# Seven-product FFN up stage in a written-out order, with the split of f moved to the down stage and eight PSUM banks for the two plain pairs

## Chip, core and metric

The kernel runs on one core of one Trainium2 chip. The metric is the device time of one execution in microseconds (us). Engines are named as in the profile: PE (TensorE matmul), PEld (its weight loads), DVE (VectorE), ACT (ScalarE), POOL (GpSimd), SP (SyncE, which here only issues loads). A name with a "q" behind it (SPq, POOLq) is that engine's queue issuing a DMA.

## What is computed

One layer of a decoder trunk on x of 1024 x 1024, float32: token mixing (dilated attention in three groups, a gated convolution branch, a gated merge, an output projection, RMSNorm), and then the channel-mixing part, which is all that the change touches:

```python
h = rms_norm(x, norm_ffn_pre[layer])
u = h @ w_up[layer].astype(h.dtype)                         # 1024 x 1024 by 1024 x 5632
u = causal_depthwise_conv(u, ffn_conv_w[layer], ffn_conv_b[layer])   # 3 taps along the sequence
u_gate, u_val = jnp.split(u, 2, axis=-1)                    # 2816 each
f = jax.nn.gelu(u_gate, approximate=True) * u_val
y = f @ w_down[layer].astype(f.dtype)                       # 1024 x 2816 by 2816 x 1024
x = x + rms_norm(y, norm_ffn_post[layer])
```

## The kernel before, in words

**Products.** Every float32 operand is split into a high part (fp32r) and a low part (the rest), and a product is the sum of three matmuls: high by high, high by low, low by high. `split` (L188 to L194) makes the parts of a weight tile: an ACT copy writes `wh` (L192), a DVE subtraction writes `wl` (L193). `wh` and `wl` have 7 buffers each.

**Up stage.** The 2816 gate and 2816 value channels are taken in 22 blocks j of 128. For one j the transposed output (256 channels by 1024 positions) is a 2 x 2 arrangement of 128 x 512 quarters, and so are its weights (`quadrant`, L714, 256 KB each, loaded by SP) and its input (the quarters B11, B21, B12, B22 of the normed and transposed h, in four chunks k). Two blocks, j = 0 and 1, are made plainly (`up_plain`, L732): eight products of 512 rows each for a block, each 12 matmuls of 128 x 512 (`product`, L723). The other 20 use seven products instead of eight (`class Seven`, L747), on sums of the quarters: T1 to T4 of the input (made once, `strassen_rows`, L150) and s1 to s4 of the weights (made by POOL for each block, L757 to L760, in `ws` tiles). I call the products of a block P1 (weights a11, L764), P5 (s1, L767), P2 (a12, L772), P6 (s2, L774), P7 (s3, L778), P3 (s4, L782) and P4 (a22, L784).

**The accumulators.** A block has one PSUM tile `pp` of 128 x 1024, with two buffers in turn. Its halves are `b1` (P1, P2, P3) and `b2` (P5, P6, P7, P4). Between the products partial results are copied out or from one half to the other: after P5 `gate` high half <- b2 (L768) and b2 <- b1 (L769); after P2 `gate` low half <- b1 (L773); after P6 b1 <- b2 (L775), all on ACT; after P7 `val` high half = b2 + gate (L779, DVE); after P3 `gate` high half += b1 (L783, DVE); after P4 `val` low half <- b2 (L785, ACT).

**Behind the products** (`gated`, L698): for the gate and the value tile an ACT scale and bias (L691) and two DVE taps (L694), then gelu on ACT (L701), a DVE product (L702), the split of f on ACT and DVE (L703, L704), and two stores of both parts into a scratch in DRAM (L706).

**Plain pairs.** Outputs of j = 0 take both halves of two `pp` tiles, those of j = 1 the two `ps` banks; a weight is loaded and split again for each half h of the positions. The results are copied into `u` tiles (L743), which live in the pool `ffn`; that pool takes the memory of the pool `res`, in which the input sums T1 to T4 are formed.

**Down stage** (`down`, L822): for each half of the positions, 22 steps k; SP loads both parts of f (512 KB, L829) and two weight quarters (L833), and 24 matmuls (L212 to L214) accumulate into all eight banks.

**What sets the order.** Before the change a scheduler puts the instructions of each engine in an order of its own by a timeline that it estimates. On the chip each engine's queue then runs in that order, and waits on semaphores for what comes from other engines.

Of the kernel before, what the change touches and what calls it, by code (L numbers as in the profile page):

```python
# [11 lines left out]
F32 = mybir.dt.float32  # L12
F32R = mybir.dt.float32r
# [65 lines left out]
def trunk_kernel(ctx: ExitStack, tc: tile.TileContext, a, out):  # L79
# [14 lines left out]
    def ps_tile(shape=(P, 512), tag=None):  # L94

        if tag is None:
            tag = ("ps", "pt", "ps", "po")[banks[0] % 4]
            banks[0] += 1
        return psum.tile(list(shape), F32, tag=tag, name=tag, bufs=2 if tag == "ps" else 1)
# [7 lines left out]
    def f(ap):  # L107
        return ap.bitcast(F32)
# [21 lines left out]
    def rsqrt_of(ss, scale, eps, pool, tag, n=1):  # L130
# [15 lines left out]
                nc.vector.tensor_mul(t, t, h)  # L146
            nc.vector.scalar_tensor_tensor(y, t, 1.5, y, op0=ALU.subtract, op1=ALU.mult)
        return y

    def strassen_rows(b11, b21, pt12, pt22, gain12, gain22, temp, make):  # L150

        def parts(x):
            t = make()
            nc.scalar.copy(t[:, 0], x)
            nc.vector.tensor_sub(t[:, 1], x, f(t[:, 0]))
            return t

        b12, b22 = temp("x12"), temp("x22")  # L160
        nc.scalar.activation(b12, pt12, AF.Copy, scale=gain12)
        nc.scalar.activation(b22, pt22, AF.Copy, scale=gain22)
        out = {"B22": parts(b22), "B12": parts(b12)}
        t1, t3, t2 = temp("x1"), temp("x3"), temp("x2")
        nc.gpsimd.tensor_sub(t3, b22, b12)
        nc.vector.tensor_sub(t1, b12, f(b11[:, 0]))
        nc.vector.tensor_sub(t1, t1, f(b11[:, 1]))
        out["T1"] = parts(t1)
        out["T3"] = parts(t3)
        nc.vector.tensor_sub(t2, b22, t1)  # L170
        out["T2"] = parts(t2)
        nc.vector.tensor_sub(t2, f(b21[:, 0]), t2)
        nc.vector.tensor_add(t2, t2, f(b21[:, 1]))
        return out, lambda: parts(t2)

    def transposed(rows, parts, gain, tag=None):

# [49 lines left out]
    with ExitStack() as mix:  # L227
# [372 lines left out]
        with tc.tile_pool(name="res", bufs=1) as res:  # L600
# [18 lines left out]
            for h in range(2):  # L619
# [32 lines left out]
                if h == 0:  # L652
# [1 line left out]
                        h2T[k] = dt(F32R, (P, 2, 512))  # L654
                    transposed(h2, lambda k: (h2T[k][:, 0], h2T[k][:, 1]), ffn_g)
                    continue
                temps = {"x12": ("xr", 0), "x22": ("xr", 1), "x1": ("oc", 0), "x2": ("oc", 1)}
                last = []
                for k in range(4):
                    pair = [ps_tile((P, 4, P), tag) for tag in ("pt", "po")]  # L660
                    for n, pt in enumerate(pair):
                        for t in range(4):
                            c = (k + 4 * n) * P
                            nc.tensor.transpose(pt[:, t, :], h2[t][:, c:c + P], ident)
                    wide = {"xr": nat2("xr", 2), "oc": nat2("oc", 1)}
                    third = res.tile([P, 512], F32, tag="x3", name="x3", bufs=2)

                    def temp(name):
                        if name == "x3":
                            return third  # L670
                        tag, n = temps[name]
                        return wide[tag][:, n * 512:(n + 1) * 512]

                    p12, p22 = (pt.rearrange("p a b -> p (a b)") for pt in pair)
                    more, t4 = strassen_rows(h2T[k], h2T[k + 4], p12, p22, ffn_g[:, k:k + 1],
                                             ffn_g[:, k + 4:k + 5], temp, lambda: dt(F32R, (P, 2, 512)))
                    for name, tile_ in more.items():
                        X[name, k] = tile_
                    X["B11", k], X["B21", k] = h2T[k], h2T[k + 4]
                    X["T4", k] = t4()  # L680


    with tc.tile_pool(name="ffn", bufs=1) as ffn:
        fscr = dram.tile([NF, 2, P, 2, 512], F32, name="fscr")

        def u_tile():
            return ffn.tile([P, S], F32, tag="u", name="u", bufs=6)

        def conv3(src, c):
            o = u_tile()  # L690
            nc.scalar.activation(o, src, AF.Identity, scale=ffn_w[:, c, 2:3], bias=ffn_b[:, c:c + 1])  # L691
            for k in (1, 0):
                d = 2 - k
                nc.vector.scalar_tensor_tensor(o[:, d:], src[:, :S - d], ffn_w[:, c, k:k + 1], o[:, d:],  # L694
                                               op0=ALU.mult, op1=ALU.add)
            return o

        def gated(j, gate, val):  # L698

            og, ov = conv3(gate, j), conv3(val, NF + j)  # L700
            nc.scalar.activation(og, og, AF.Gelu_apprx_tanh)  # L701
            nc.vector.tensor_mul(og, og, ov)  # L702
            nc.scalar.copy(ov.bitcast(F32R), og)  # L703
            nc.vector.tensor_sub(og.bitcast(F32R), og, ov)  # L704
            for n, src in enumerate((ov, og)):
                nc.gpsimd.dma_start(fscr[j, :, :, n, :].rearrange("h p c -> p h c"),  # L706
                                    src.rearrange("p (h c) -> p h c", h=2))

        def raw_tile(early=False):
            if early:  # L710
# [21 lines left out]
        def up_plain(js):  # L732

            us = {(j, c): u_tile() for j in js for c in range(2)}
            pps = {c: pp_tile() for c in range(2)}
            for h in range(2):
                for n, j in enumerate(js):
                    for c in range(2):
                        ps = pps[c][:, h * 512:(h + 1) * 512] if n == 0 else ps_tile(tag="ps")
                        for kh in range(2):  # L740
                            product(ps, wsplit(quadrant(j, 2 * c + kh)), ("B11", "B21", "B12", "B22")[2 * h + kh], kh == 0, kh == 1)
                        dst = us[j, c][:, h * 512:(h + 1) * 512]
                        (nc.vector.tensor_copy if c else nc.scalar.copy)(dst, ps)  # L743
            for j in js:
                gated(j, us[j, 0], us[j, 1])

        class Seven:  # L747

            def __init__(self, j):
                self.j = j
                self.a11, self.a21, self.a22, self.a12 = (quadrant(j, q) for q in (0, 2, 3, 1))
                self.s = [ffn.tile([P, 512], F32, tag="ws", name="ws", bufs=4) for _ in range(4)]
                s1, s2, s3, s4 = self.s
                nc.gpsimd.tensor_add(s1, self.a21, self.a22)  # L757
                nc.gpsimd.tensor_sub(s2, s1, self.a11)
                nc.gpsimd.tensor_sub(s3, self.a11, self.a21)
                nc.gpsimd.tensor_sub(s4, self.a12, s2)  # L760
                both = pp_tile()
                self.b1, self.b2 = both[:, 0:512], both[:, 512:1024]
                self.gate, self.val = u_tile(), u_tile()
                product(self.b1, wsplit(self.a11), "B11", True, False, True)  # L764

            def fifth(self):
                product(self.b2, wsplit(self.s[0]), "T1", True, False, True)  # L767
                nc.scalar.copy(self.gate[:, 512:1024], self.b2)  # L768
                nc.scalar.copy(self.b2, self.b1)  # L769

            def second(self):
                product(self.b1, wsplit(self.a12), "B21", False, False, True)  # L772
                nc.scalar.copy(self.gate[:, 0:512], self.b1)  # L773
                product(self.b2, wsplit(self.s[1]), "T2", False, False, True)  # L774
                nc.scalar.copy(self.b1, self.b2)  # L775

            def seventh(self):
                product(self.b2, wsplit(self.s[2]), "T3", False, False, True)  # L778
                nc.vector.tensor_add(self.val[:, 512:1024], self.b2, self.gate[:, 512:1024])  # L779

            def last(self):
                product(self.b1, wsplit(self.s[3]), "B22", False, False, True)  # L782
                nc.vector.tensor_add(self.gate[:, 512:1024], self.b1, self.gate[:, 512:1024])  # L783
                product(self.b2, wsplit(self.a22), "T4", False, False, True)  # L784
                nc.scalar.copy(self.val[:, 0:512], self.b2)  # L785
                gated(self.j, self.gate, self.val)

        up_plain((0, 1))
        now = Seven(2)
        now.fifth()  # L790
        for j in range(2, NF):
            now.second()
            then = Seven(j + 1) if j + 1 < NF else None
            now.seventh()
            if then:
                then.fifth()
            now.last()
            now = then


        post = dt()
# [20 lines left out]
        def down(h, late=3):  # L822
# [2 lines left out]
            banks += [[ps_tile(tag="ps") for _ in range(2)], [ps_tile(tag=tag) for tag in ("pt", "po")]]  # L825

            def load(k):
                ft = dt(F32R, (P, 2, 512))
                nc.sync.dma_start(f(ft), fscr[k, h])  # L829
                w = []  # L830
                for cs in cols:
                    raw = raw_tile()
                    nc.sync.dma_start(raw, a["w_down"][k * P:(k + 1) * P, cs])  # L833
                    w.append(wsplit(raw))
                return ft, w
# [87 lines left out]
```

## Time and profile before

| what | us |
|---|---|
| median of 3 runs (1889.32 to 1891.16) | 1889.87 |
| the profiled execution | 1892.74 |
| its span, first to last instruction | 1891.0 |
| PE busy in the span | 1782.0 |
| DVE busy | 1187.2 |
| ACT busy | 720.7 |
| POOL busy | 217.7 |

A row of the timeline has the start, the duration, the engine, the line, the operation, what it writes <- reads and a count of merged instructions; in brackets stands how long the engine was idle before and which instruction released it. Matmuls overlap, so one of 390 ns starts every 227 ns when PE is fed. PEclk is the granted clock of TensorE: 1.00 is 2.4 GHz, 0.50 is 1.2 GHz.

### The profile page before, as it was taken

What the parts mean: (1) busy time and instruction counts of PE and PEld (TensorE: products, weight loads), DVE (VectorE), ACT (ScalarE), POOL (GpSimd) and SP (SyncE); (2) the same over time, 40 slices, a digit from 0 to 9 for tenths busy, and PEclk for the clock granted to TensorE, in tenths of its full rate; (3) what the DMA queues carried; (4) which work ended last, traced back from release to release, by engine and by line L of the source; (5) the groups of instructions that cost most, each with busy time, mean ns of one, the idle gap of its engine ahead of it and who ended that gap; (6) DMA issues with size and microseconds to landing.
All of it is one profiled execution on the core that took longest, in us unless ns stands there. A gap on an engine that the chain in (4) does not pass through costs nothing. (4 is left out here: it accounts for less than half of the span.)

```text
span 1891.0 us, 22339 instructions
## 1 busy us (share of the span) xinstructions
PE 1782.0 (94%) x8152; PEld 1488.4 (79%) x8152; DVE 1187.2 (63%) x1956; ACT 720.7 (38%) x1312; POOL 217.7 (12%) x211
## 2 busy tenths in 40 slices
PE   7799998999999999999999994899999999999997
PEld 5688898888888888888888883777777777888886
DVE  6249978367752969657644578766666666532624
ACT  6132343333323342223432444455454545422322
POOL 0000000111100000000000001433333333000000
PEclk9899999999999999999999997999999999999999
DMA  5312132112321222354331431432222232885522
GB/s 188 105 48 59 48 93 79 52 53 61 90 61 54 57 68 89 101 175 131 98 112 59 148 125 48 135 102 109 90 100 89 90 122 89 309 325 172 181 92 101
DMA packets 87246, 203.68 MB, mean 108 GB/s; under 512 B 11347, under 2 KB 13283, under 8 KB 87136
## 3 DMA queue, kind: packets, MB, share of 16 engines
q1 hardware_dynamic: 72000, 159.42, 26.4%
q0 software_dynamic: 11888, 39.26, 6.2%
q10 hardware_dynamic: 3248, 3.58, 0.6%
q8 instruction: 64, 1.05, 0.2%
q14 instruction: 46, 0.38, 0.1%
HBM read 155.93 MB, written 48.38 MB: 108 GB/s over the span
## 5 line engine op out<-in xcount | busy, mean ns | idle before, releaser
L212 PE MATMUL pp<-d,wh 128*128 128x512 f32 x1088 | 429.8, 395 | 15.9 <-DVE d L358 15.6
L729 PE MATMUL pp<-d,wh 128*128 128x512 f32 x1184 | 377.2, 400 | 61.7 <-DVE u L779 31.9
L214 PE MATMUL pp<-d,wl 128*128 128x512 f32 x1088 | 428.8, 394 | 0.0
L213 PE MATMUL pp<-d,wh 128*128 128x512 f32 x1088 | 428.7, 394 | 0.0
L729 PEld LDWEIGHTS pp<-d,wh 128*128 128x128 f32 x1184 | 226.5, 193 | 118.1 <-DVE u L779 40.0
L297 DVE SCALAR_TENSOR_TENSOR acc<-cin,conv_w,acc 128x1024 f32<-128x1024 f32 x240 | 304.9, 1279 | 4.5 <-issue 1.4
L212 PEld LDWEIGHTS pp<-d,wh 128*128 128x128 f32 x1088 | 206.0, 189 | 58.7 <-issue 16.6
L193 DVE TENSOR_TENSOR wl<-wr,wh 128x512 fp32r<-128x512 f32 x207 | 142.2, 691 | 162.5 <-ACT wh L192 162.1
L214 PEld LDWEIGHTS pp<-d,wl 128*128 128x128 f32 x1088 | 206.1, 189 | 41.7
L213 PEld LDWEIGHTS pp<-d,wh 128*128 128x128 f32 x1088 | 206.1, 189 | 41.2
L729 PE MATMUL pp<-d,wl 128*128 128x512 f32 x592 | 235.4, 398 | 0.0
L192 ACT CAST wh<-wr 128x512 fp32r<-128x512 f32 x207 | 127.7, 621 | 279.4 <-PE pp L213 164.3
L193 DVE TENSOR_TENSOR wl<-wq,wh 128x512 fp32r<-128x512 f32 x148 | 122.2, 832 | 148.0 <-ACT wh L192 146.6
L192 ACT CAST wh<-wq 128x512 fp32r<-128x512 f32 x148 | 91.8, 623 | 221.3 <-PE pp L214 119.3
L694 DVE SCALAR_TENSOR_TENSOR u<-u,ffn_w 128x1023 f32<-128x1023 f32 x88 | 113.7, 1292 | 53.0 <-ACT u L691 53.0
L729 PEld LDWEIGHTS pp<-d,wl 128*128 128x128 f32 x592 | 114.3, 193 | 24.6
L192 ACT CAST wh<-ws 128x512 fp32r<-128x512 f32 x80 | 49.3, 618 | 119.8 <-PE pp L729 119.8
L212 PE MATMUL pp<-wh,d 128*128 128x512 f32 x232 | 90.2, 391 | 0.7 <-ACT oc L637 0.7
L213 PE MATMUL pp<-wl,d 128*128 128x512 f32 x232 | 90.4, 390 | 0.0
L214 PE MATMUL pp<-wh,d 128*128 128x512 f32 x232 | 90.4, 390 | 0.0
L351 PE MATMUL pp<-wh,d 128*128 128x512 f32 x192 | 79.5, 415 | 3.0 <-DVE d L358 3.0
L352 PE MATMUL pp<-wl,d 128*128 128x512 f32 x192 | 78.3, 408 | 0.0
(282 smaller groups left out, 2549.9 us busy)
## 6 DMA issues: line engine op xcount, KB each, us to landing
fscr<-u POOLq DMA_DIRECT2D x44, 512.0 KB, 4.9
d<-fscr SPq DMA_DIRECT2D x44, 512.0 KB, 7.2
wq<-in_w_down_dram SPq DMA_DIRECT2D x88, 256.0 KB, 3.1
wq<-in_w_up_dram SPq DMA_DIRECT2D x80, 256.0 KB, 3.2
wr<-in_w_v_dram SPq DMA_DIRECT2D x48, 256.0 KB, 2.8
wr<-in_w_qk_dram SPq DMA_DIRECT2D x48, 256.0 KB, 2.7
wr<-in_w_glu_dram SPq DMA_DIRECT2D x32, 256.0 KB, 2.7
wr<-in_w_gate_dram SPq DMA_DIRECT2D x32, 256.0 KB, 2.8
```

The lines of the kernel that those rows point to most:

```text
L192: nc.scalar.copy(hi, raw)
L193: nc.vector.tensor_sub(lo, raw, f(hi))
L212: nc.tensor.matmul(ps, lh, rh, start=first, stop=False)
L213: nc.tensor.matmul(ps, lh, rl, start=False, stop=False)
L214: nc.tensor.matmul(ps, ll, rh, start=False, stop=last)
L297: nc.vector.scalar_tensor_tensor(acc, cin[:, k:k + S], conv_w[:, m, k:k + 1], acc, op0=ALU.mult, op1=ALU.add)
L351: nc.tensor.matmul(ps, hTh[k][:, sl], wh, start=k == 0, stop=False)
L352: nc.tensor.matmul(ps, hTh[k][:, sl], wl, start=False, stop=False)
L694: nc.vector.scalar_tensor_tensor(o[:, d:], src[:, :S - d], ffn_w[:, c, k:k + 1], o[:, d:], op0=ALU.mult, op1=ALU.add)
L729: nc.tensor.matmul(ps, wp[:, cs], xp, start=first and k == 0 and n == 0, stop=last and k == 3 and n == 2, skip_group_check=open_)
```

## The change

- **Order.** The up stage of the 20 blocks is no longer left to the scheduler. `Seven.steps` gives each action a slot (`AT` for the products, one product a slot, seven slots a block) and a rank in it (product and the copies behind it 0, loads 1, weight split 2, POOL sums 3, what follows the products 4). All actions are sorted by slot, rank and block, and issued under `tc.manual_schedule()`, which keeps each engine's queue in the issued order. A weight is split five slots ahead of its product; a22 is loaded a second time. The order of products stays P2, P6 of a block, P1 of the next, P7, P5 of the next, P3, P4.
- **f.** L703 and L704 are gone from the up stage; f goes to the scratch once, as float32 (512 KB for each block in place of 1 MB), and the down stage loads 256 KB for a step and splits it there, on ACT and DVE, out of a `ws` tile.
- **Plain pairs.** j = 1 uses `ps`, `ps` in the first half of positions and `pt`, `po` in the second. Seven of the eight split weights are kept for the second half.
- **Input sums.** B12 and B22 of all four chunks are made first, in `d` tiles, and T1 to T4 after them, with two `xr` buffers in place of one `oc`.

```diff
-                temps = {"x12": ("xr", 0), "x22": ("xr", 1), "x1": ("oc", 0), "x2": ("oc", 1)}
...
+                        x = wide[k][:, n * 512:(n + 1) * 512]
+                        nc.scalar.activation(x, pt.rearrange("p a b -> p (a b)"), AF.Copy, scale=ffn_g[:, c:c + 1])
+                        X[("B12", "B22")[n], k] = parts(x)
...
+                for k in range(4):
+                    b12, b22 = wide[k][:, 0:512], wide[k][:, 512:1024]
+                    both = nat2("xr", 2)
+                    t1, t3 = both[:, 0:512], both[:, 512:1024]
+                    nc.vector.tensor_sub(t1, b12, f(h2T[k][:, 0]))
+                    nc.vector.tensor_sub(t1, t1, f(h2T[k][:, 1]))
+                    X["T1", k] = parts(t1)
+                    nc.gpsimd.tensor_sub(t3, b22, b12)
+                    X["T3", k] = parts(t3)
+                    nc.vector.tensor_sub(t1, b22, t1)
+                    X["T2", k] = parts(t1)
+                    nc.vector.tensor_sub(t1, f(h2T[k + 4][:, 0]), t1)
+                    nc.vector.tensor_add(t1, t1, f(h2T[k + 4][:, 1]))
+                    X["T4", k] = parts(t1)
...
-            nc.scalar.copy(ov.bitcast(F32R), og)
-            nc.vector.tensor_sub(og.bitcast(F32R), og, ov)
...
-                        ps = pps[c][:, h * 512:(h + 1) * 512] if n == 0 else ps_tile(tag="ps")
+                        ps = pps[c][:, h * 512:(h + 1) * 512] if n == 0 else ps_tile(tag=("ps", "ps", "pt", "po")[2 * h + c])
                         for kh in range(2):
-                            product(ps, wsplit(quadrant(j, 2 * c + kh)), ("B11", "B21", "B12", "B22")[2 * h + kh], kh == 0, kh == 1)
+                            key = j, 2 * c + kh
+                            if h == 0 or key not in kept:
+                                w = wsplit(quadrant(*key))
+                                if len(kept) < 7:
+                                    kept[key] = w
+                            else:
+                                w = kept[key]
+                            product(ps, w, ("B11", "B21", "B12", "B22")[2 * h + kh], kh == 0, kh == 1)
...
+        WEIGHT = {"P1": "a11", "P2": "a12", "P3": "s4", "P4": "a22", "P5": "s1", "P6": "s2", "P7": "s3"}
+        OPERAND = {"P1": "B11", "P2": "B21", "P3": "B22", "P4": "T4", "P5": "T1", "P6": "T2", "P7": "T3"}
+        AT = {"P1": 2, "P5": 4, "P2": 7, "P6": 8, "P7": 10, "P3": 12, "P4": 13}
+        AHEAD = 5
...
+            def multiply(self, p):
+                if p == "P1":
+                    both = pp_tile()
+                    self.b1, self.b2 = both[:, 0:512], both[:, 512:1024]
+                b = self.b1 if p in ("P1", "P2", "P3") else self.b2
+                product(b, self.t[p], OPERAND[p], p in ("P1", "P5"), False, True)
+                lo, hi = slice(0, 512), slice(512, 1024)
+                if p == "P5":
+                    self.gate = u_tile()
+                    nc.scalar.copy(self.gate[:, hi], b)
+                    nc.scalar.copy(self.b2, self.b1)
+                elif p == "P2":
+                    nc.scalar.copy(self.gate[:, lo], b)
+                elif p == "P6":
+                    nc.scalar.copy(self.b1, self.b2)
+                elif p == "P7":
+                    self.val = u_tile()
+                    nc.vector.tensor_add(self.val[:, hi], b, self.gate[:, hi])
+                elif p == "P3":
+                    nc.vector.tensor_add(self.gate[:, hi], b, self.gate[:, hi])
+                elif p == "P4":
+                    nc.scalar.copy(self.val[:, lo], b)
...
+            def taps_gate(self):
+                taps(self.og, self.gate, self.j)
+                nc.scalar.activation(self.og, self.og, AF.Gelu_apprx_tanh)
...
+                yield from ((AT[p], 0, lambda p=p: self.multiply(p)) for p in AT)
+                yield from ((AT[p] - AHEAD, 2, lambda p=p: self.split(p)) for p in AT)
+                for at, name, q in ((-5, "a21", 2), (-5, "a22", 3), (-5, "a11", 0), (0, "a12", 1), (5, "a22", 3)):
+                    yield at, 1, lambda name=name, q=q: self.load(name, q)
+                for at, *args in ((-3, "s1", "tensor_add", "a21", "a22"), (-2, "s3", "tensor_sub", "a11", "a21"),
+                                  (-1, "s2", "tensor_sub", "s1", "a11"), (3, "s4", "tensor_sub", "a12", "s2")):
+                    yield at, 3, lambda args=args: self.sum_(*args)
+                for at, what in ((12, self.scale_gate), (13, self.taps_gate), (13, self.scale_val),
+                                 (14, self.taps_val), (15, self.join), (16, self.store)):
+                    yield at, 4, what
...
+        todo = [(7 * n + at, rank, n, what) for n in range(NF - 2) for at, rank, what in Seven(n + 2).steps()]
+        with tc.manual_schedule():
+            for *_, what in sorted(todo, key=lambda x: x[:3]):
+                what()
...
             def load(k):
+                raw = ffn.tile([P, 512], F32, tag="ws", name="ws", bufs=4)
+                nc.sync.dma_start(raw, fscr[k][:, h * 512:(h + 1) * 512])
                 ft = dt(F32R, (P, 2, 512))
-                nc.sync.dma_start(f(ft), fscr[k, h])
+                nc.scalar.copy(ft[:, 0], raw)
+                nc.vector.tensor_sub(ft[:, 1], raw, f(ft[:, 0]))
```

## Rows read from the trace of the kernel before

**Rows 1.** Page: busy time of each engine, share of the span, instructions.
```profile
PE 1782.0 (94%) x8152; PEld 1488.4 (79%) x8152; DVE 1187.2 (63%) x1956; ACT 720.7 (38%) x1312; POOL 217.7 (12%) x211
```
**Rows 2.** Windows: stretch, its us, busy us and count by engine, PEclk, DMA.
```profile
1130.40:1208.20 77.80, 49.40 (x223) 40.16 (x222) 62.27 (x109) 38.78 (x69) 18.31 (x12) 0.82 0.24 78
1208.20:1651.50 443.30, 409.38 (x1730) 330.82 (x1729) 296.08 (x305) 223.65 (x322) 142.07 (x116) 0.97 0.36 124
...
1660.00:1878.00 218.00, 218.00 (x963) 180.50 (x963) 79.37 (x173) 60.84 (x110) 1.46 (x2) 1.00 0.51 175
```
**Rows 3.** Waits of PE, 1208 to 1652: who waits <- for whom, us, times, longest.
```profile
PE pp L729 <- DVE u L779: 31.9, 19, 1.8
```
**Rows 4.** Timeline at the end of the plain pairs' stall.
```profile
1183.41 0.69 DVE L157 TENSOR_TENSOR d<-oc,d 128x512 fp32r<-128x512 f32 x1 [0.68 <-ACT d L156]
1184.13 0.58 ACT L743 COPY u<-pp 128x512 f32<-128x512 f32 x1 [0.76 <-DVE d L157]
1184.24 2.79 SPq L717 DMA_DIRECT2D wq<-in_w_up_dram  x5
...
1184.77 1.22 PE L729 MATMUL pp<-d,wh 128*128 128x512 f32 x2 [27.82 <-ACT u L743]
```
**Rows 5.** Timeline of a steady block, where PE stops.
```profile
1402.13 1.88 DVE L704 TENSOR_TENSOR u<-u 128x1024 fp32r<-128x1024 f32 x1 [0.57 <-ACT u L703]
...
1402.50 0.39 PE L729 MATMUL pp<-d,wl 128*128 128x512 f32 x1
...
1403.93 0.68 DVE L779 TENSOR_TENSOR u<-pp,u 128x512 f32<-128x512 f32 x1
...
1404.67 0.50 PE L729 MATMUL pp<-d,wh 128*128 128x512 f32 x1 [1.78 <-DVE u L779]
```
**Rows 6.** Timeline of the first seven-product block (P2, P6, P7, P3 in succession).
```profile
1222.30 0.58 ACT L773 COPY u<-pp 128x512 f32<-128x512 f32 x1
...
1222.93 0.73 PE L729 MATMUL pp<-d,wh 128*128 128x512 f32 x2 [0.97 <-ACT u L773]
...
1230.09 0.69 DVE L779 TENSOR_TENSOR u<-pp,u 128x512 f32<-128x512 f32 x1 [2.94 <-PE pp L729]
...
1230.84 0.73 PE L729 MATMUL pp<-d,wh 128*128 128x512 f32 x2 [0.84 <-DVE u L779]
```
**Rows 7.** Groups by line, 1208 to 1651: count, busy us, mean ns, idle before.
```profile
L694 DVE SCALAR_TENSOR_TENSOR u<-u,ffn_w 128x1023 f32<-128x1023 f32 x82 | 105.0, 1280 | 49.2 <-ACT u L691 49.2
...
L193 DVE TENSOR_TENSOR wl<-ws,wh 128x512 fp32r<-128x512 f32 x78 | 56.0, 718 | 2.8 <-ACT wh L192 2.8
L691 ACT ACTIVATE u<-u,ffn_b,ffn_w 128x1024 f32<-128x1024 f32 x40 | 49.5, 1238 | 8.0 <-DVE u L783 7.9
L192 ACT CAST wh<-ws 128x512 fp32r<-128x512 f32 x78 | 48.1, 618 | 119.5 <-PE pp L729 119.5
...
L701 ACT ACTIVATE u<-u 128x1024 f32<-128x1024 f32 x20 | 21.3, 1064 | 3.1 <-DVE u L694 3.1
...
L785 ACT COPY u<-pp 128x512 f32<-128x512 f32 x19 | 11.0, 579 | 0.0
```
**Rows 8.** Windows: two periods of a block; first and last of four long stops, with what followed.
```profile
1272.50:1293.60 21.10, 19.32 (x85) 15.69 (x84) 14.63 (x16) 11.14 (x16) 7.46 (x7) 1.00 0.29 100
1293.60:1316.40 22.80, 21.02 (x85) 16.83 (x84) 14.77 (x16) 11.12 (x16) 7.49 (x7) 0.93 0.28 93
...
290.40:293.80 3.40, 0.91 (x6) 0.50 (x5) 3.40 (x6) 1.76 (x4) 0.00 (x0) 1.00 0.29 80
293.81:297.22 3.41, 3.41 (x15) 3.15 (x14) 3.41 (x6) 1.45 (x3) 0.00 (x0) 0.50 0.00 0
...
537.20:539.50 2.30, 0.35 (x2) 0.03 (x1) 2.30 (x4) 1.59 (x3) 0.00 (x0) 1.00 0.37 114
539.58:546.39 6.81, 5.82 (x14) 4.60 (x15) 4.43 (x6) 0.59 (x1) 0.00 (x0) 0.50 0.12 39
```
**Rows 9.** Windows: the stretch in which the input sums are made.
```profile
1147.70:1184.10 36.40, 8.68 (x48) 6.63 (x46) 33.15 (x47) 19.27 (x35) 7.09 (x4) 0.68 0.05 15
```

## Prediction made before the changed kernel was run

> **What bounds the kernel now.** I read the page first: PE is busy for 1782 of 1891.0 us [rows 1], so only what makes PE stop can be gained. Then the windows by stage [rows 2]: in the down stage, from 1660 to 1878 us, PE is busy throughout at full clock, and nothing is to be won. It starts 963 matmuls in 218.0 us there: 0.2264 us each, 2.72 for a product of twelve. The up stage has the stops. Its plain part has PE busy for 49.4 of 77.8 us; its seven-product part makes 1730 matmuls in 443.3 us where they want 391.7, and so loses 51.6 us.
>
> The waits say to whom [rows 3]: 19 stops behind L779, the DVE add that empties b2 after P7. The timeline shows why it is late [rows 5]: DVE runs its queue in order, L704 (the low part of f, itself waiting for ACT) stands in front and ends at 1404.0, and L779 starts only then, although P7's last matmul was over at 1402.9. PE stops 1.78 us; start to start that is 2.17 in place of 0.23 (a stop costs its idle time and 0.16), and in the timeline the second matmul comes another 0.11 late, so 2.05 us a block. Some stops are followed by a stretch of 3.4 us at half clock: a period of seven products and one stop takes 21.1 us at PEclk 1.00 and some 22.7 where such a stretch falls into it [rows 8], 1.6 us more. PEclk 0.97 over 443.3 us answers to about seven of these [rows 2]. So 51.6 is 17 x 2.05 + 7 x 1.6 and about 5 at the two ends.
>
> The plain part's stop is 27.8 us long [rows 4]. PE waits for the copy L743 of a finished half; this copy writes the first `u` tile, and it starts right behind the last instruction of the input sums (L157 at 1183.4), together with the first loads into `wq`, which had nothing else to wait for. I read this as: pool `ffn` opens when pool `res` is done, and that stays so.
>
> **Which wait decides.** In the first block P2, P6, P7 and P3 ran in direct succession, and show what the half tiles are worth [rows 6]. L773 reads b1; P6 writes b2; yet P6 starts 0.05 us after L773 ends, with PE idle 0.97 us. L779 reads b2; P3 writes b1; yet P3 waits for it, 0.84 us. So a product waits until every earlier read of either half of its tile is done. The changed code has the same tile with the same halves, and in its order P6 follows P2 with nothing between, and P4 follows P3. The old queue had put another block's product in each of these two places.
>
> The Trainium skill, page "PSUM — Partial Sum Buffer", section "PSUM bank collisions raise a hardware error", says that engines on different banks do not collide and that guarding by bank is enough. By that rule P6 and P4 would not have to wait at all; the rows above show that in this program they do. It is the first rival below.
>
> **The change, part by part.**
>
> *P3 to P4.* P3 ends, DVE adds b1 into `gate`, P4 starts. The row of L779 with DVE free [rows 6]: idle 0.84 us, and 0.16 + 0.11 as above, 1.11 us. Twenty blocks: 22 us.
>
> *P2 to P6.* Here the copy of b1 is on ACT, and what counts is what stands before it in ACT's written queue. In P4's slot (13) that is, in rank order: the copy of `val`'s low half (waits for P4's end), the split of a weight, the gelu of this block, the scale of `val`. In the next slot comes the copy behind P2 of the next block. The gelu waits for `taps_gate` on DVE, and in DVE's slot 13 the low part of the same split stands before the taps, which itself waits for ACT's high part, which waits behind the copy, which waits for P4. So from P4's end everything is one chain [rows 7]: copy 0.58, L192 0.62, L193 0.69 to 0.72, two taps 2 x 1.28, gelu 1.06, scale 1.24, copy 0.58: 7.3 us, and I add 0.1 for eight hand-overs (0.03 to 0.1 us each, partly given back where instructions of one engine overlap by 0.08). P6 would otherwise start 2.56 us after P4's end (P2 takes 2.72, and its first matmul starts before P4's last is out). The stop is 7.36 - 2.56 = 4.8 us, and 0.11 behind it: 4.9 us. It comes in 19 of 20 blocks: 93 us. The wait stands in ACT's queue; behind it queue this slot's weight split and the copy for P6, and PE waits for these in turn, but they have slack (P1 of the next block covers 2.7 us). From below: if the taps did not queue behind the split, the chain would be 5.3 us or so, the stop 2.9. From above: DVE subtractions that run beside POOL's sums take up to 1.1 us longer, 4.9 + 1.1.
>
> *Clock.* Longer stops than 1.8 us are in the trace elsewhere [rows 8]: of four, 2.3 to 3.0 us idle, all were followed by PEclk 0.50, three for 3.4 us and the last for 6.8. A half-speed stretch full of work loses half of itself, 1.7 us; one that begins inside the stop less. I take the 1.6 us measured between the two periods, 19 times: 30 us. Bounds: none (0), and 2.9 each (55).
>
> *Ends.* In the first block P2 follows P5 at once and waits for two ACT copies (1.4 us), and P6 follows P2 with no gelu in the queue (0.97 + 0.27); with what the last block exposes, 4 us.
>
> *What goes.* All of the 51.6 us: L703 and L704 leave the queues of ACT and DVE, and between P7 and P3 stands P5 of the next block, 2.72 us of cover for an add that needs 0.8. So the seven-product part loses 22 + 93 + 30 + 4 = 149 in place of 51.6: **+98 us**.
>
> *Plain pairs and input sums.* The 44 DVE instructions remain. In 36.4 us DVE was busy for 33.15 [rows 9], and two buffers in place of one let chunks overlap, so most of the other 3.2 can go: I put their end at 1181. Until then PE can now run also what goes to `pt` and `po`, once B12 and B22 are ready (16 ACT and 8 DVE instructions of 0.6 to 0.7 us from 1147.7, so about 1159 by durations like those of [rows 7]); only four products (10.9 us) need the copies from the `pp` halves and come after. The plain part ends at 1181 + 0.7 + 10.9 + 1.6 = 1194 in place of 1208: **-14 us**. If the queue of PE has the four in front, all nine left come after the copies and nothing is won; with the sums done at 1178 it is -17. Saved splits (9 in place of 16) are under the stop anyway.
>
> *f in the down stage.* A step of 24 matmuls is 5.4 us; ACT gets 0.62 more and DVE 0.7 beside loads that bring half the bytes. DVE was busy 79 and ACT 61 of 218 us there [rows 2], so PE covers it: 0. If the cover is gone where the stages meet, some 5 us. Half the stores in the up stage: off the chain, 0.
>
> **Sum.** 1892.74 + 98 - 14 = 1977 for an execution like the profiled one. The median of the runs lies 2.87 us below that one: **1974 us**, 4.5% slower.
>
> **Rivals.**
> 1. *The halves are guarded by bank* (the case of the page's rule). P6 and P4 then follow at once. The chain of 7.3 us still delays ACT, and P7 has to wait for the copy b1 <- b2, some 0.7 us a block: 15 + 4 lost in place of 51.6, and -14: 1889.9 - 33 - 14 = **1843**. It ends on the other side, and decides from where both stops of a block together, with their half-clock, cost less than 3.1 us ((51.6 + 14 - 4) / 20). Against: [rows 6].
> 2. *The written order does not bind ACT and DVE behind one another as listed*, so that the copy behind P2 comes promptly: each block loses 1.24 + 1.11, 47 us and 4, with no long stop and no half clock: 1889.9 - 0.6 - 14 = **1875**. For: the old queues had gelu and scale between such copies without harm, because another product covered them. Against: the ranks, gelu before the next slot.
> 3. *The clock stays up*: my forecast without 30 us, **1944**. For: 10 of 17 stops of 1.78 us had no half-speed stretch. Against: all four longer stops had one.
>
> **How the numbers follow.** My forecast with the clock 0.76, rival 3 0.09, rival 1 0.07, rival 2 0.05, and 0.03 for losses that just meet the gains. The first two have one sign. The range takes in rival 3 with the larger gain of the plain part and somewhat shorter chains (1935), and the upper bounds of clock and POOL together in part (2005). About 0.2% is what a measurement of this kernel can tell from no change: faster 0.12, same 0.02, slower 0.86.
>
> **What would show it.** Right: in the waits PE behind the ACT copy after P2, 19 or 20 times, near 4.6 us each (idle, without pipeline), with the taps, gelu and scale of the block before in front of it on the timeline; PE behind the DVE add after P3, 20 times 0.8; a period near 26.7 us; PEclk near 0.5 for 3.4 us in each; no wait for the add after P7; the plain part's stop in two pieces, together near 15 us. Wrong: products in direct succession across P2 and P6, or an idle time there under 1 us; then rival 1 or 2. A single plain stop near 28 us would mean that PE's queue has the four products in front.

## The result, and the profile after

The changed kernel takes 2014.33 us (median of 4 runs, 2011.59 to 2016.20) beside 1889.59 us of the kernel before (1889.04 to 1891.16): 1.0658 times as long, 95% interval 1.0639 to 1.0676. The profiled execution took 2014.27 us with a span of 2012.5. The forecast of 1974 had the sign and placed the two stops of a block; it was 40 us short, and the time lies above the range (1935 to 2005).

PE's waits in the profile after (who waits for whom: us in total, times, longest):

```profile
PE pp L704 <- ACT u L770: 84.7, 20, 4.5
PE pp L704 <- ACT u L726: 18.0, 1, 18.0
PE pp L704 <- DVE u L777: 16.9, 19, 1.1
...
PE pt L186 <- ACT d L850: 11.6, 1, 11.6
...
PE pp L704 <- ACT pp L768: 6.9, 1, 6.9
```

In this kernel L770 is the copy of b1 behind P2, L777 the add behind P3, L726 the first copy of the plain pairs, L850 the split of f in the down stage, and L768 the copy b2 <- b1 behind P5. The wait of [rows 3], for the add behind P7, is gone. The first and third lines are the two stops that the forecast placed. One of them in the timeline of a steady block (start, length, engine, line, operation, and in brackets the idle time before it and what ended that):

```profile
1263.29 0.59 ACT L779 COPY u<-pp 128x512 f32<-128x512 f32 x1 [1.88 <-PE pp L704]
...
1263.77 0.62 ACT L166 CAST wh<-ws 128x512 fp32r<-128x512 f32 x1
...
1264.43 0.69 DVE L167 TENSOR_TENSOR wl<-ws,wh 128x512 fp32r<-128x512 f32 x1 [3.70 <-ACT wh L166]
...
1265.04 2.60 DVE L681 SCALAR_TENSOR_TENSOR u<-u,ffn_w 128x1023 f32<-128x1023 f32 x2
...
1267.72 1.06 ACT L789 ACTIVATE u<-u 128x1024 f32<-128x1024 f32 x1 [3.33 <-DVE u L681]
1268.69 1.23 ACT L675 ACTIVATE u<-u,ffn_b,ffn_w 128x1024 f32<-128x1024 f32 x1
1269.82 0.56 ACT L770 COPY u<-pp 128x512 f32<-128x512 f32 x1
...
1270.43 1.22 PE L704 MATMUL pp<-d,wh 128*128 128x512 f32 x2 [4.46 <-ACT u L770]
```

Read it downwards: the copy of `val`, high part of a weight, its low part, two taps, gelu, scale of `val`, and only then the copy for which PE waits. It is the chain of the forecast, link by link, 7.1 us from 1263.29 to PE's start at 1270.43. Now the clock round that stop, and a whole period (windows: stretch, its us, PE busy, PEclk, DMA share, GB/s; the last line has PE, PEld, DVE, ACT and POOL):

```profile
1266.00:1268.80 2.80, 0.00 (x0) 1.00 0.00 0
1268.80:1270.43 1.63, 0.00 (x0) 0.50 0.00 0
1270.43:1275.20 4.77, 4.77 (x11) 0.50 0.00 0
1275.20:1275.64 0.44, 0.44 (x2) 0.51 0.00 0
1275.64:1284.00 8.36, 8.36 (x38) 1.00 0.43 133
...
1257.11:1284.44 27.33, 21.99 (x86) 17.38 (x85) 12.31 (x14) 9.88 (x16) 5.69 (x5) 0.88 0.24 69
```

The clock falls to its lower level while PE stands idle and comes back 6.8 us later; 5.2 us of these lie on P6, where half is lost. The same happens at all 19 long stops, so the period is 27.33 us where [rows 8] had 21.1 and 22.8.

**Where the time went.** I count what each stretch takes above 0.2267 us for each of its matmuls (transposes left out):

| stretch | before | after | difference | forecast |
|---|---|---|---|---|
| plain part, from 1130 to its last matmul | 34.7 | 26.3 | -8.4 | -14 |
| seven-product part | 51.5 | 168.7 | +117.2 | +98 |
| down stage and end | 11.1 | 24.4 | +13.4 | 0 |

Together +122 us, as the spans have it (+121.5). In the seven-product part 10.8 us lie at the first block and 19 periods lose 8.30 each (27.34 less 84 matmuls, 19.04).

The down stage has a stop that was not there before, where its second half begins. Timeline, SP's issues first (it issues the stores of the output too, and not only loads), then what PE waits for:

```profile
1864.75 1.00 SPq L839 DMA_DIRECT2D out_dram<-u  x2
...
1871.79 0.91 SPq L855 DMA_DIRECT2D wq<-in_w_down_dram  x2
1872.75 2.59 SPq L848 DMA_DIRECT2D ws<-fscr  x4
...
1879.47 2.62 ACT L850 CAST d<-ws 128x512 fp32r<-128x512 f32 x4 [6.27 <-DMA ws<-fscr]
...
1880.14 0.80 PE L186 MATMUL pt<-wh,d 128*128 128x512 f32 x1 [11.62 <-ACT d L850]
```

The first load of f for the second half is issued at 1872.75, after the last matmuls of the first half, and lands at 1879.47. Its destination `ws` is the tag from which the epilogue takes the tiles for its squares.

### The profile page after: what moved, and what is told of

It reads as the page before. It is cut to its first block, busy times and chain, and to the rows that moved or that the text cites. A ratio compares the mean times of both kernels' runs of the same rounds, so it can differ in the third digit from the quotient of the medians.

```text
span 2012.5 us, 22135 instructions
## 1 busy us (share of the span) xinstructions
PE 1825.5 (91%) x8152; PEld 1514.5 (75%) x8152; DVE 1164.7 (58%) x1971; ACT 713.5 (35%) x1327; POOL 180.8 (9%) x189
## 4 chain that ended last, share of the span: by engine, by line
PE 56%; issue 26%; DVE 8%; ACT 5%; DMA 3%; POOL 2%; ACTq 1%; SPq 0%; POOLq 0%; DVEq 0%
PE pp L704 19%; PE pp L186 9%; PE pp L187 9%; PE pp L188 9%; DVE u L681 3%; DVE wl L167 1%; PE ps L186 1%; ACT u L675 1%; PE ps L188 1%; PE ps L187 1%; ACT u L789 1%; DMA ws<-fscr 1%; ACT wh L166 1%; DVE u L777 1%; POOL oscr L416 1%
## 5 line engine op out<-in xcount | busy, mean ns | idle before, releaser
L704 PE MATMUL pp<-d,wh 128*128 128x512 f32 x1184 | 407.2, 428 | 127.2 <-ACT u L770 84.7
L186 PE MATMUL pp<-d,wh 128*128 128x512 f32 x1088 | 429.9, 395 | 14.9 <-DVE d L332 14.7
L188 PE MATMUL pp<-d,wl 128*128 128x512 f32 x1088 | 429.0, 394 | 0.0
L187 PE MATMUL pp<-d,wh 128*128 128x512 f32 x1088 | 428.9, 394 | 0.0
L704 PEld LDWEIGHTS pp<-d,wh 128*128 128x128 f32 x1184 | 243.1, 209 | 196.8 <-ACT u L770 93.5
L186 PEld LDWEIGHTS pp<-d,wh 128*128 128x128 f32 x1088 | 206.1, 189 | 57.5 <-issue 15.7
L704 PE MATMUL pp<-d,wl 128*128 128x512 f32 x592 | 248.4, 420 | 0.0
L188 PEld LDWEIGHTS pp<-d,wl 128*128 128x128 f32 x1088 | 206.1, 189 | 41.7
L187 PEld LDWEIGHTS pp<-d,wh 128*128 128x128 f32 x1088 | 206.2, 190 | 41.2
L167 DVE TENSOR_TENSOR wl<-wq,wh 128x512 fp32r<-128x512 f32 x148 | 102.6, 702 | 227.1 <-ACT wh L166 227.1
L167 DVE TENSOR_TENSOR wl<-wr,wh 128x512 fp32r<-128x512 f32 x200 | 136.5, 686 | 154.7 <-ACT wh L166 152.9
L166 ACT CAST wh<-wr 128x512 fp32r<-128x512 f32 x200 | 123.4, 621 | 269.6 <-PE pp L187 166.0
L704 PEld LDWEIGHTS pp<-d,wl 128*128 128x128 f32 x592 | 123.0, 208 | 28.0
L167 DVE TENSOR_TENSOR wl<-ws,wh 128x512 fp32r<-128x512 f32 x80 | 63.2, 790 | 129.6 <-ACT wh L166 129.6
L681 DVE SCALAR_TENSOR_TENSOR u<-u,ffn_w 128x1023 f32<-128x1023 f32 (+1 forms) x88 | 113.3, 1290 | 7.0 <-ACT u L675 5.6
```

The costliest lines, as they stand in the source:

```text
L166: nc.scalar.copy(hi, raw)
L167: nc.vector.tensor_sub(lo, raw, f(hi))
L186: nc.tensor.matmul(ps, lh, rh, start=first, stop=False)
L187: nc.tensor.matmul(ps, lh, rl, start=False, stop=False)
L188: nc.tensor.matmul(ps, ll, rh, start=False, stop=last)
L704: nc.tensor.matmul(ps, wp[:, cs], xp, start=first and k == 0 and n == 0, stop=last and k == 3 and n == 2, skip_group_check=open_)
```

## The experiments

`gelu_later`, `fill_stop` and `f_own_ring` were executed once. The changed kernel's own runs lie between 2011.59 and 2016.20 us, so for these three I also give what the edited part takes in the two traces.

**Two tiles in place of two halves.** Only the allocation changes; each half was a bank before and is one now.

```
-                    both = pp_tile()
-                    self.b1, self.b2 = both[:, 0:512], both[:, 512:1024]
+                    self.b1 = ps_tile(tag="ps")
+                    self.b2 = ps_tile(tag=("pt", "po")[self.j % 2])
```

> The changed kernel, with b1 and b2 of a block as two tiles of one bank each in place of two halves of one. Theory (a product waits for the readers of the whole tile): the stops P2 to P6 (4.46 us idle) and P3 to P4 (0.88 us idle) are gone with their half clock, a period goes from 27.34 to about 19.8 us, P7 waits some 0.7 us for the copy b1 <- b2; time near 2014 - 150 = 1864 us. Rival (the products wait because ACT and DVE touch the bank's memory or because of the written order itself, whatever the tile): the stops stay, 2014 us.

Measured 1864.39 us, 0.987 times the kernel before (0.984 to 0.990). Windows of PE, one from P2 of a block to P2 of the next and one over most of the blocks, then rows of the timeline (P6, the copy of b1, the copy b1 <- b2, P7):

```profile
1310.04:1329.42 19.38, 19.34 (x86) 1.00 0.31 96
1215.00:1589.00 374.00, 371.29 (x1612) 1.00 0.30 98
...
1312.76 0.62 PE L704 MATMUL po<-d,wh 128*128 128x512 f32 x2
...
1316.78 0.56 ACT L770 COPY u<-ps 128x512 f32<-128x512 f32 x1
...
1317.76 0.58 ACT L772 COPY ps<-po 128x512 f32<-128x512 f32 x1
...
1318.40 0.73 PE L704 MATMUL po<-d,wh 128*128 128x512 f32 x2
```

The stops of 4.46 and 0.88 us are gone. A period takes 19.38 us, 0.34 more than its 84 matmuls (19.04): P7 still follows the copy b1 <- b2, which reads the tile that P7 writes, but this costs 0.3 us and not the 0.7 that the expectation had. So the wait of P6 is one for the tile, and not for the bank or for the order: with the same order and the same reads, P6 starts 4.0 us before the copy of b1, as soon as the two lie in tiles of their own. This also settles the point on which the trace and the Trainium skill stood against each other in the prediction. The Trainium skill's page "PSUM — Partial Sum Buffer", section "PSUM bank collisions raise a hardware error", is borne out for the banks (ACT's copy of b1 at 1316.78 reads one bank while PE writes another, and neither waits), and the wait of [rows 6] was the program's own, for the shared tile.

**The chain in ACT's queue.** The gelu is taken out of the taps' step, and it and all that follows it come one slot later (the new step itself is left out here); the tile stays shared.

```
-                for at, what in ((12, self.scale_gate), (13, self.taps_gate), (13, self.scale_val),
-                                 (14, self.taps_val), (15, self.join), (16, self.store)):
+                for at, what in ((12, self.scale_gate), (13, self.taps_gate), (14, self.gelu), (14, self.scale_val),
+                                 (15, self.taps_val), (16, self.join), (17, self.store)):
```

> The changed kernel, with the gelu and the scale of val one slot later (14), so that in ACT's queue they stand behind the copy of b1; taps of gate stay in slot 13. Theory (the 4.46 us are the chain taps, gelu, scale in front of the copy): the stop P2 to P6 falls to about 0.97 us idle, P3 to P4 stays at 0.88, the half clock goes too, a period of about 21.4 us; time near 2014 - 119 = 1895 us. If the half clock stays although the stops are short: some 2.4 us more a block, 1943. Rival (it is not the queue order): no change, 2014.

Measured 1905.42 us. The copy now stands in front of the gelu (ACT and PE in the timeline, then a period in the windows):

```profile
1255.54 0.62 ACT L166 CAST wh<-ws 128x512 fp32r<-128x512 f32 x1
1257.83 0.59 ACT L770 COPY u<-pp 128x512 f32<-128x512 f32 x1 [1.67 <-PE pp L704]
1258.31 0.62 ACT L166 CAST wh<-ws 128x512 fp32r<-128x512 f32 x1
1260.39 1.06 ACT L791 ACTIVATE u<-u 128x1024 f32<-128x1024 f32 x1 [1.46 <-DVE u L681]
...
1258.46 0.73 PE L704 MATMUL pp<-d,wh 128*128 128x512 f32 x2 [0.73 <-ACT u L770]
...
1252.00:1273.20 21.20, 19.61 (x84) 15.61 (x84) 14.42 (x15) 9.93 (x16) 7.15 (x6) 1.00 0.26 87
```

The stop falls from 4.46 to 0.73 us and the clock stays up: two stops of 0.73 and 0.88 us a period bring no half clock. The time is 10 us above what I expected, and the seven-product part is 106.6 us shorter in the trace than in the changed kernel. The steady periods are right (21.2); nearly all of the rest lies in the last block, where the down stage's first splits of f run between the block's own instructions and PE waits 2.0, 1.6 and 3.5 us.

**The clock by itself.** 18 matmuls that nobody reads fill the stop; ACT and DVE do what they did.

```
                 elif p == "P2":
                     nc.scalar.copy(self.gate[:, lo], b)
+                    spare = ps_tile(tag="ps")
+                    for n in range(18 if self.j > 2 else 0):
+                        nc.tensor.matmul(spare, self.t[p][0][:, 0:P], X["B21", 0][:, 0], start=n == 0, stop=n == 17)
```

> The changed kernel, with 18 matmuls that nobody reads (4.1 us at full clock) into a spare bank between P2 and P6 of each block but the first, so that most of the 4.46 us stop is filled with TensorE work while ACT and DVE do what they did. Theory (the stop itself brings the half clock, 2.4 us a block): the wait of P6 falls to some 0.4 us idle, P6 starts as late as before, PEclk rises to near 1.00, a period of about 24.9 us; time near 2014 - 46 = 1968. Rival (the half clock comes from something else in the block): the period stays 27.3 or grows to some 30 if the added matmuls run at half clock; 2014 to 2070.

Measured 1966.68 us: TensorE does 342 matmuls more and the kernel is 47.7 us faster; the seven-product part alone is 44.8 us shorter in the trace. A period in the windows of PE, and the start of P6 in a timeline:

```profile
1229.70:1254.65 24.95, 23.69 (x102) 1.00 0.25 74
...
1264.88 0.74 PE L704 MATMUL pp<-d,wh 128*128 128x512 f32 x2 [0.39 <-ACT u L770]
```

The period is 24.95 in place of 27.34, with the chain as long as before. So 2.4 us of each block, 19 x 2.4 = 46 us in all, were the half clock, and they came from the stop.

**f's loads in a ring of their own.** The down stage takes f's raw tile from tag `wr`.

```
-                raw = ffn.tile([P, 512], F32, tag="ws", name="ws", bufs=4)
+                raw = raw_tile(True)
                 nc.sync.dma_start(raw, fscr[k][:, h * 512:(h + 1) * 512])
```

> The changed kernel, with the loads of f in the down stage in the buffers of tag wr (free by then) in place of tag ws, which they share with the squares of the epilogue. Theory (the 12 us stop where the two halves of the down stage meet is that shared ring): stop and its half clock gone, 2014 - 14 = 2000. Rival (the loads are late because of their place in SP's queue behind the stores of the output): no change, 2014.

Measured 2000.23 us, 14.1 less; in the traces the matmuls of the down stage take 228.6 us in place of 242.0. The wait for L850 is gone from PE's list, and PE works through the meeting of the halves (windows of PE, then SP's last load of f and its first store of the output):

```profile
1860.00:1880.00 20.00, 20.00 (x90) 1.00 0.66 219
...
1809.96 0.33 SPq L848 DMA_DIRECT2D wr<-fscr  x1
...
1863.34 1.00 SPq L839 DMA_DIRECT2D out_dram<-u  x2
```

The scheduler, which still orders the down stage, now issues all 44 loads of f before the first store of the output; in the changed kernel the loads of the second half stood behind the first stores. So the stop came with the shared ring, by its buffers and by the later place in SP's queue that goes with them; no run parts these two. It cost 13 to 14 us, a little more than its own 11.6.

**Each part alone, and the order away.** Three kernels. The first is the kernel before with f split in the down stage, without the written order and with the old plain pairs:

```
-            nc.scalar.copy(ov.bitcast(F32R), og)
-            nc.vector.tensor_sub(og.bitcast(F32R), og, ov)
...
+            nc.gpsimd.dma_start(fscr[j], og)
...
```

> The kernel before, with f split in the down stage alone (one store of f, L703 and L704 gone, f's raw tile in tag ws as in the changed kernel); order by the scheduler. Theory: nothing stands in front of L779 any more, so the 17 stops of 1.78 us and their half clock go (46 us); the meeting of the two halves of the down stage gets its 12 us stop (14 with the clock): 1889 - 46 + 14 = 1857. Rival: the scheduler sets other DVE work in front of L779, the stops stay: 1903.

Measured 1877.49 us, 0.9935 (0.9916 to 0.9953). PE's waits:

```profile
PE pp L725 <- DVE u L775: 15.4, 19, 1.2
...
PE pt L212 <- ACT d L827: 11.7, 1, 11.7
```

L775 is here the add behind P7. The rival did not come, nothing stands in front of the add; but the stop did not go either. It fell from 1.78 to 0.785 us, the bare add, since P3 follows P7 at once and both write halves of one tile. 18 stops, each with 1.09 us lost (the period is 20.13 and the products want 19.04), are the 20 us that the expectation lacks.

The second is the kernel before with the new input sums and plain pairs alone (the change of the banks is shown):

```
...
-            pps = {c: pp_tile() for c in range(2)}
+            pps = [pp_tile() for c in range(2)]
...
-                        ps = pps[c][:, h * 512:(h + 1) * 512] if n == 0 else ps_tile(tag="ps")
+                        ps = pps[c][:, h * 512:(h + 1) * 512] if n == 0 else ps_tile(tag=("ps", "ps", "pt", "po")[2 * h + c])
...
```

> The kernel before, with the new input sums, the eight banks and the kept weights of the two plain pairs alone. The forecast gave this part -14; the trace of the changed kernel, by its lost time up to the end of the plain pairs, gives about -8: 1881. Rival: the four products behind the stop take back what is won: 1889.

Measured 1887.16 us, 0.9987 (0.9975 to 1.0000): at most a quarter of a per cent, and perhaps nothing. Its waits say where the gain goes:

```profile
PE pp L738 <- ACT u L760: 18.0, 1, 18.0
...
PE pp L738 <- ACT pp L786: 5.1, 1, 5.1
```

The plain pairs end at 1199.4 in place of 1208.2, and then P2 of the first block waits for the copy b2 <- b1 (L786 here). ACT comes to it at 1214.86, right behind the second plain pair's gelu, which starts at 1213.30. In the changed kernel the same stop is the 6.9 us of L768: the gelu starts at 1209.69, the two copies at 1210.65 and 1211.25. (By the code the first of them writes `gate`, the next of six `u` tiles, which the gating of the plain pairs must also let go; no run parts the queue from the ring.) By the start of the 277th matmul of the up stage the lead has shrunk from 8.8 us to 1.2 (1230.84 before, 1229.67 here).

The third is the changed kernel with its steps handed to the scheduler.

```
-        with tc.manual_schedule():
-            for *_, what in sorted(todo, key=lambda x: x[:3]):
-                what()
+        for *_, what in sorted(todo, key=lambda x: x[:3]):
+            what()
```

> The changed kernel without the written-out order: the same steps are handed to the scheduler, both halves of a block's banks stay one tile. Theory (the stops come from the order together with the shared tile): the scheduler sets products of another block into the two places, the stops of 4.5 and 0.9 us go for the most part: 1850 to 1875 us. Rival (the steps of one product themselves cost the time): 2014.

Measured 1874.57 us, 0.9916 (0.9896 to 0.9936). The 4.46 us stop is gone (PE's waits):

```profile
PE pp L704 <- DVE u L775: 15.5, 19, 1.3
```

With the same steps and the same tile, the written order alone costs 2014.3 - 1874.6 = 140 us: the scheduler leaves one place in a block where two products of one tile meet, with 0.78 us, and the written order has two, one of them with a chain of eight instructions in front.

**Put together.** First the two mends (two tiles, f in `wr`) with the written order:

> The changed kernel with b1 and b2 as tiles of their own and f's raw tiles in tag wr; the gating of the plain pairs where the change has it. If the moved gating cost the combined kernel time (its up stage ended 2.5 us later than that of separate tiles alone), this one is faster than its 1854: 1864 - 14.5 = 1850. If not, 1854 or more.

Measured 1857.12 us, 0.9827 (0.9804 to 0.9849). The mends add up to less than expected: the up stage ends 4.7 us later than with two tiles alone. In the last block f's splits are ready sooner and go in between on ACT (timeline):

```profile
1588.44 0.56 ACT L770 COPY u<-ps 128x512 f32<-128x512 f32 x1
1588.91 0.62 ACT L166 CAST wh<-ws 128x512 fp32r<-128x512 f32 x1
1589.43 1.66 ACT L850 CAST d<-wr 128x512 fp32r<-128x512 f32 x3
1590.99 0.58 ACT L772 COPY ps<-po 128x512 f32<-128x512 f32 x1
```

PE waits 3.5 us for that last copy. With two tiles alone it waited 2.9 us there and no half clock followed; here 6.8 us at half clock do, and PE stops twice more, for 0.9 and 1.6 us (windows of PE, `sep_banks` and then `two_mends`):

```profile
1589.87:1596.00 6.13, 6.13 (x27) 1.00 0.65 213
...
1590.74:1597.57 6.83, 5.95 (x14) 0.50 0.51 166
```

With the gating of the second plain pair moved behind P5 of the first block:

```
...
+            scale_(0, 0), scale_(0, 1), taps_(0, 0), taps_(0, 1), gelu_(0), join_(0)
+            return [(5, 4, -1, lambda: scale_(1, 0)), (5, 4, -1, lambda: taps_(1, 0)), (6, 4, -1, lambda: gelu_(1)),
+                    (6, 4, -1, lambda: scale_(1, 1)), (7, 4, -1, lambda: taps_(1, 1)), (8, 4, -1, lambda: join_(1))]
...
```

> The changed kernel with b1 and b2 as tiles of their own, f's raw tiles in tag wr, and the gating of the second plain pair put behind P5 of the first block in the written order, so that the first copy into gate no longer waits for its taps. From the 1864 of the separate tiles: -14 for the meeting of the down halves, -5 of the 7.2 us stop ahead of P2 of the first block: 1845. Rival for the last part: the copy waits for the taps of the first plain pair as long, 1850.

Measured 1854.34 us, 0.9810 (0.9794 to 0.9827). The stop ahead of P2 falls from 7.0 to 1.3 us, and one of 4.2 us ahead of P7 takes its place; beside the two mends that is 2.8 us less, and their runs overlap (up to 1855.65 here, from 1855.19 there), so that I leave open whether the move gains anything.

And the two mends without the written order:

> As the kernel with the two mends, without the written-out order. Theory (the 0.78 us stop between P7 and P3 in each block, 20.13 us a period, is the shared tile as well): with two tiles it goes, period 19.04: 1874.6 - 14.5 - 18 x 1.09 = 1840. Rival (the written order is needed once the tiles are apart: the scheduler's own order brings other waits): 1850 or more.

Measured 1841.58 us, 0.9738 (0.9722 to 0.9755): the fastest of all, 48 us below the kernel before and 173 below the change. Windows of all engines, 350 us of the blocks:

```profile
1230.00:1580.00 350.00, 350.00 (x1546) 289.79 (x1545) 247.03 (x270) 198.03 (x292) 98.05 (x86) 1.00 0.33 105
```

PE does not stop there. That answers both sides of its expectation: the 0.78 us stop of the scheduler's order was the shared tile as well, and once the tiles are apart the written order is not needed.

## Why the prediction was right or wrong, point by point

Two terms failed: the price of the half clock behind the long stop (30 us in the sum, 45 measured), and f in the down stage (0 in the sum, 13 measured). Without either one of these two misses, 15 and 13 us, the time would have lain inside the range, which ended at 2005. The places and lengths of the two stops held.

- **Which wait decides**: right. P6 after P2 and P4 after P3 wait for the readers of the whole tile; `sep_banks` shows it by taking the tile away, and 150 us with it. Rival 1, halves guarded by bank, fell. Its price of 1843 comes near the 1864 of two tiles once 14 us of the down stage and 6 of the plain part are added, but partly by luck: of its 15 us for P7's wait only some 6 came (0.3 us a block), while the first block and the last lost about 13 where it had 4.
- **The two stops**: right in place, number and size. P2 to P6 4.46 us idle for 4.6, 18 times, with 0.73 in the first block and 3.67 in the last; P3 to P4 0.88 for 0.84, 19 times. `gelu_later` shows that the 4.46 us are the chain.
- **Clock**: the mechanism was right (rival 3 fell, every long stop had its half clock), and this is the term that was mis-sized: 1.6 us a block in the forecast, 2.4 measured, 15 us over 19 blocks. I took the price from stops of 1.78 us, where 3.4 us of half clock followed; here it lasts 6.8 us, as at the last of the long stops in [rows 8], and 1.6 of them fall into the stop. That row was quoted and its price not taken. The length of a stop would not have told which price to take: the last two of the four long stops were equally long (timeline of the kernel before), and the first of them had 3.4 us of half clock, the second 6.8. What decides between them, no run shows. The bound I gave, 2.9, held the measured 2.4.

```profile
512.48 0.79 PE L351 MATMUL pp<-wh,d 128*128 128x512 f32 x1 [3.02 <-DVE d L358]
...
540.57 0.77 PE L212 MATMUL pp<-d,wh 128*128 128x512 f32 x1 [3.02 <-DVE d L358]
```

- **Ends**: mis-sized, 4 us forecast and 10.8 at the first block. The wait for two ACT copies was put at 1.4 us, as if ACT were free; the gating of the plain pairs stands in its queue until 1210.75, and the stop is 6.9 us, with a half clock behind it. I had followed the queue in the steady block and not in the first. Whether the ring of `u` tiles would have held the copy as long, no run shows.
- **f in the down stage**: the wrong step. It was costed at 0 with "some 5 us" if the cover went where the stages meet. The cover that went lies where the two halves of the down stage meet, and it went because the raw tile of f came into a ring that the epilogue uses: 13.4 us in the down stage, which `f_own_ring` gives back. The bytes and the DVE and ACT work were counted, the buffers not.
- **Plain pairs**: -14 forecast, -8.4 up to their last matmul. I let most of DVE's 3.2 us of idle time go; of 36.4 us before the end of the sums DVE was busy for 30.2 in the profile after and 33.2 before, and it waited 4.1 us for ACT's high parts, six times up to 0.7; by the code each sum of a chunk is made from the one before. The sums ended at 1185.94 instead of 1181, later than before (1184.10). What was won lies in front: twelve of the sixteen products ran ahead of the stop where eight had before, and four were left behind it (before, eight were left, not the nine of the forecast). Of these 8.4 us nearly all is paid back at the first block, as `plain_alone` shows.
- **What goes**: right for the add behind P7 in the written order, where P5 of the next block covers it; `f_alone` shows that taking L703 and L704 away alone would have left 0.785 us of it.
- **Range**: the misses are 15 (clock), 7 (first block), 13 (down stage) and 6 (plain part), less 3 by which the two stops together came out shorter: 38 us between profiled executions. The other 2 to 3 are the 2.87 us by which I set the median below the profiled execution; of the changed kernel the two agree. The upper end, 2005, held the clock's bound in part and no bound for f in the down stage, where a price of 5 us stood in the text.

## What to carry to other kernels

When an order is written by hand, list for each pair of neighbouring products which tile they share, not which bank, and what stands in the copying engine's queue ahead of the copy that frees it; give accumulators that are read at different times tiles of their own. When a load moves into an existing tag, look up every other user of the tag and the time at which the last of them lets go. A stop is priced with the clock that follows it; where like stops in the trace have two prices, as 3.4 and 6.8 us of half clock behind 3.02 us here, the range takes in the dearer one in full.

## What the runs showed of the hardware that I had not expected

- Work that nobody reads made the kernel 47.7 us faster (`fill_stop`): PE's granted clock was 1.00 over a period with stops of 0.39 and 0.88 us, and 0.88 with stops of 4.46 and 0.88 us.
- In the changed kernel the clock falls in the stop and not after it: 1.00 for 2.8 us of standing still, then 0.50 for the last 1.6 us of it and for 5.2 us of work. In the kernel before it fell after the stop: one of 1.78 us ended at 1295.80, and the clock was 0.50 from 1297.33 on.
- The length of a stop did not settle what followed it. Stops of 0.73 and 0.88 us brought no half clock in `gelu_later`; of the 17 stops of 1.78 us seven did, in the kernel before and in `plain_alone` alike; one of 2.9 us did not in `sep_banks`; behind stops of 3.5 us it lasted 3.4 us in `gelu_later` and `combined` and 6.8 in `two_mends`.
- A DVE subtraction of 128 x 512 that ran beside a sum of POOL took 1.7 to 1.8 us, and 0.7 us otherwise, in the same stretch of the changed kernel:

```profile
1164.65 1.60 POOL L658 TENSOR_TENSOR xr<-d 128x512 f32<-128x512 f32 x1 [12.45 <-DVE d L635]
1165.03 1.77 DVE L655 TENSOR_TENSOR xr<-d,d 128x512 f32<-128x512 f32 x1
...
1167.92 0.68 DVE L656 TENSOR_TENSOR xr<-xr,d 128x512 f32<-128x512 f32 x1
```
